# Two transformer blocks on one core: the adaptive modulation computed in three places, partly on VectorE

## Chip, core and metric

One core of a Trainium2 chip runs the whole kernel in a single launch. The metric is device time in microseconds, the median of several executions. TensorE multiplies matrices, VectorE and ScalarE do elementwise work and empty the accumulators, GpSimd does some elementwise work and issues some loads, SyncE issues the other loads. Matmul results go to eight accumulator banks.

## The reference

Two blocks run one after the other on 256 tokens of width 1024. The first block has a norm, a wide projection, a stick-breaking attention, an RWKV recurrence, gates over both, an output projection `w_o` and an FFN. The second block is modulated by a vector `c` that doesn't depend on the tokens:

```
def modulate(x, shift, scale):
    return rms_norm_2(x) * (1 + scale[:, None, :]) + shift[:, None, :]

# first block, cut
gates = sigmoid(proj[..., SB_COLS + RW_COLS:] + b_gate)
merged = gates[..., :D] * (o_sb @ w_sb_out) + gates[..., D:] * (o_rw @ w_rw_out)
x = x + rms_norm(merged @ w_o, norm_mix_post)
h = rms_norm(x, norm_ffn_pre)
x = x + rms_norm((silu(h @ w_ffn_gate) * (h @ w_ffn_up)) @ w_ffn_down, norm_ffn_post)
# second block, cut
mod = jax.nn.silu(c) @ w_ada + b_ada            # (1024) @ (1024 x 6144)
sh1, sc1, g1, sh2, sc2, g2 = jnp.split(mod, 6, axis=-1)
proj = modulate(x, sh1, sc1) @ w_in             # then pooling and a state space mixer
x = x + g1 * mix
x = x + g2 * hier_moe(modulate(x, sh2, sc2))    # 32 experts, two for each token
return rms_norm_2(x) * final_norm_w
```

## The kernel before

The code is written in the order of the computation, with tiles taken from pools. A scheduler that knows the dependences and the number of buffers then fixes an order of instructions for each engine before the launch; each engine works through its own list in that order and waits where an input or a buffer isn't ready. The stages are: first norm; projections of the RWKV part (`prw`); projections q, k and v of the attention (`pqk`, `pv`); attention, RWKV recurrence and gates (`pgate`, 16 column blocks) mixed with each other; output projections of both branches (`psb`, `prw`); `w_o` by rows with its norm (`fin_mix`); FFN in 22 groups (`pfg`, `pfu`); FFN down with its norm (`fin_ffn`); second block; router; 32 experts whose weights (192 MB) stream in.

Products in high precision are made from two rounded parts: `split_to` and `wsplit` have ScalarE cast a weight to `wh` and VectorE subtract to get `wl`, and `mm3` issues three matmuls.

`w_ada` is stored as 24 blocks of 256 columns, 1 MB each, with the 1024 rows as 8 groups of 128 in one tile. `mod_steps` handles a pair of blocks: GpSimd issues the two loads into the two buffers of the tag `wada`, TensorE makes 8 products for each block into a bank `pmod` (in four strips of 32 rows), ScalarE copies it to `modrow`, TensorE transposes the copy in four parts, and VectorE sums the four strips and adds `b_ada`. The result is four columns of `modT`, which holds the whole modulation as columns of 128. It is called twelve times: once after each of the four projections of q and k, and once after each of the eight gate weights `wg`.

Accumulator banks are split over three tags: m (`pm`), t (`pt_`) and s (`psm`). During the first block up to `w_o` m has two, t three and s three. Projections, `pmod` and half of the accumulators of `w_o` use m; attention scores `pz`, transposes `pwt`, attention outputs `po`, `prw` of the output projection and the other half of `w_o` use t; norms, RWKV and transposes use s. From the FFN on m and s have four each, and `pt_` takes m.

`dense_rows` runs a product over rows of the weight, keeps the last weights, finishes the first 128 tokens (`finish(0, ...)`), then multiplies the kept weights for the other 128, calls `fill` if there is one, and finishes them. For the FFN down product `fill` is `router_prep`, which prepares the router's bias and the rows `g2h` and `g1row`:

```
        finish(0, acc[0])
        for k, hi, lo in kept:
            go(1, k, hi, lo)
        if fill:
            fill()
        finish(1, acc[1])
```

Of the kernel before, what the change touches and what calls it, by code (L numbers as in the profile page):

```python
# [8 lines left out]
F32 = mybir.dt.float32  # L9
# [52 lines left out]
AFT = (9, 12)  # L62
SCW = 4
WARM = (16, 4, 5, 2, 9)
PN = "mttt"
XC, W1 = 512, 2
RWE = "pp" + "d" * 12
QE = "d" * 8
# [5 lines left out]
def two_blocks(ctx: ExitStack, tc: tile.TileContext, a: dict, out: bass.AP, dump=None, stop=""):  # L74
# [16 lines left out]
    def open_banks(*banks):  # L91
        if "pst" in ph:
            ph["pst"].close()
        ph["pst"] = ExitStack()
        ph["p"] = ph["pst"].enter_context(tc.tile_pool(name="psum%d" % banks[0], bufs=1, space=PSUM))
        ph["banks"] = banks
# [11 lines left out]
    def nm(s):  # L108
        uid[0] += 1
        return f"{s}{uid[0]}"  # L110
# [31 lines left out]
    def psm(s):  # L142
        return bank(s, 2)
# [7 lines left out]
    def pconst(s, shape, dt=F32):  # L151
        return ph["pool"].tile(shape, dt, tag=s, name=s, bufs=1)

    open_banks(2, 3, 3)
    open_phase("mixing")


# [9 lines left out]
    def row_bcast(s, src, q=sync):  # L167
        t = blk(s)
        q.dma_start(out=t, in_=src.to_broadcast([P, D]))
        return t  # L170
# [43 lines left out]
    def prm(name, i=0, n=1):  # L214
        o = sum(m for x, m in PARAMS[: [x for x, _ in PARAMS].index(name)])
        return par[:, o + i : o + i + n]
# [81 lines left out]
    def split_to(hi, lo, src, eng=dve):  # L298

        act.copy(hi, src)  # L300
        eng.tensor_tensor(lo, src, hi.bitcast(F32), ALU.subtract)  # L301
# [5 lines left out]
    def atv(t, k, c0=0, c1=256):  # L307
        return t[k // 4][:, (k % 4) * 256 + c0 : (k % 4) * 256 + c1]
# [68 lines left out]
    def mod_steps():  # L377


        i = mod_n[0]  # L380
        mod_n[0] += 2
        ps = pm("pmod")
        for b in range(2):
            t = ph["pool"].tile([P, 2048], F32, tag="wada", name=nm("wada"), bufs=2)
            pool.dma_start(out=t, in_=a["w_ada_2"][i + b])
            v = t.rearrange("p (k c) -> p k c", k=KC)
            for k in range(KC):
                g = k % 4
                pe.matmul(ps[32 * g : 32 * g + 32, b * 256 : b * 256 + 256], lhsT=csil[:, k : k + 1].to_broadcast([P, 32]), rhs=v[:, k], start=(k < 4), stop=(k >= 4))
        row = small("modrow", [P, 512], bufs=1)  # L390
        act.copy(row, ps)
        for q in range(4):
            pe.transpose(ps[:, q * P : (q + 1) * P], row[:, q * P : (q + 1) * P], ident)
        sm = small("mods", [P, 4])
        dve.tensor_reduce(sm, ps.rearrange("p (q g r) -> p q g r", q=4, g=4)[:, :, :, 0], axis=AX.X, op=ALU.add)
        dve.tensor_tensor(modT[:, 2 * i : 2 * i + 4], sm, prm("b_ada_2", 2 * i, 4), ALU.add)


    hT = act_T("hT")
# [414 lines left out]
    for g in range(8):  # L814
        v = load_cols(w_in, 13 + g, 256, KC, "wg")
        for j in range(2):
            ps = pm("pgate")
            dense_T(v, KC, hT, j, P, ps[:, :256], on(GTE, 2 * g + j))
            act.activation(hv(gt[g // 2], 2 * (g % 2) + j), ps[:, :256], AF.Sigmoid, bias=prm("b_gate", 2 * g + j))
        mod_steps()  # L820
    mT = act_T("mT", blk)
    for g in range(2):
        wsb = load_cols(a["w_sb_out"], g, 512, 4, "wsb")
# [97 lines left out]
        kept_o.append(0)  # L921
        return (gblk if len(kept_o) <= 8 else blk)(s_, F32R)

    dense_rows(a["w_o"], KC, mT, fin_mix, SO, keep_o, pos=PO)

    close_phase()

# [3 lines left out]
    NF = 22  # L931
    r2 = pconst("r2", [P, 256])
    fT = [[ph["pool"].tile([P, 1024], F32R, tag=f"f{i}{j}", name=f"f{i}{j}", bufs=1) for j in range(6)] for i in range(2)]
    for g in range(NF):
        t = raw("wff")
        sync.dma_start(out=t, in_=a["w_ffn"][g])
        vs = [t[:, j * 1024 : j * 1024 + 1024].rearrange("p (k c) -> p k c", k=KC) for j in range(2)]
        p1, p2 = pm("pfg"), pt_("pfu")
        dense_T(vs[0], KC, h2T, 0, P, p1[:, :256])
        dense_T(vs[1], KC, h2T, 0, P, p2[:, :256], alloc=lambda s_: blk(s_, F32R))  # L940
        while later:
            fin_mix2(*later.pop(0))
        sl = small("ffs", [P, 256], bufs=2)
        dve.tensor_tensor(sl, p1[:, :256], r2, ALU.mult)
        act.activation(sl, sl, AF.Silu)
        dve.tensor_tensor(sl, sl, p2[:, :256], ALU.mult)
        split_to(atv(fT[0], g), atv(fT[1], g), sl)
    gfp = row_bcast("gfp", a["norm_ffn_post"])


# [38 lines left out]
    def router_prep():  # L989
        ps = psm("prb")  # L990
        for k in range(KC):
            pe.matmul(ps[:, 0:40], lhsT=sh2(k).to_broadcast([P, P]), rhs=wrt[:, k], start=(k == 0), stop=(k == KC - 1))
        dve.tensor_tensor(rbias, rbias, ps[:, 0:40], ALU.add)
        pool.tensor_tensor(wrt, wrt, sc1p[:, 8:16].rearrange("p (k o) -> p k o", o=1).to_broadcast([P, KC, 40]), ALU.mult)

        ps = psm("prow")
        for j in range(4):
            for h in range(2):
                c = 40 + 4 * h + j
                pe.matmul(ps[64 * h : 64 * h + 64, j * P : (j + 1) * P], lhsT=modT[:, c : c + 1].to_broadcast([P, 64]), rhs=ident, start=True, stop=True)  # L1000
        act.copy(g2h, ps)
        g1.append(row_of("g1row", modT[:, 16:24]))
# [729 lines left out]
```

## Time and profile before

| | us |
|---|---|
| median of three runs (1136.47 to 1138.24) | 1136.75 |
| profiled execution | 1135.27 |
| its span | 1133.5 |
| TensorE busy | 1061.0 (94%) |
| VectorE busy | 569.6 (50%) |
| ScalarE busy | 406.5 (36%) |
| GpSimd busy | 80.2 (7%) |

Busy shares are averages over stages with different limits; what bounds a stage is read from the waits in that stage. TensorE has two lines, PE for matmuls and PEld for weight loads, and matmuls overlap each other, so the distance from one start to the next tells what one costs. A product of plain f32 data appears as two records.

### The profile page before, as it was taken

To read this page: it belongs to the slowest core of one execution; us is meant where nothing else is said; L and a number is where in the kernel's file an instruction comes from. 1 tells how busy PE (TensorE), PEld (TensorE's weight loads), DVE (VectorE), ACT (ScalarE), POOL (GpSimd) and SP (SyncE) were. 2 spreads that over 40 slices of the span, in tenths; PEclk is the share of its full clock that TensorE was granted. 3 is DMA by queue.
4 is the path that set the end of the run, shared out by engine and by line. 5 is a ranking of instruction groups with operands and counts; after the bars stand their busy time and mean duration, and the time that the engine had idled before them with its cause. 6 is when DMAs were issued, how large, how long until landed. Compare 5 with 4: busy or idle time off the path is not lost.

```text
span 1133.5 us, 17717 instructions
## 1 busy us (share of the span) xinstructions
PE 1061.0 (94%) x7134; PEld 736.8 (65%) x7134; DVE 569.6 (50%) x1164; ACT 406.5 (36%) x717; POOL 80.2 (7%) x155
## 2 busy tenths in 40 slices
PE   8999999889869999999999889999999999999995
PEld 7988777778769999887997653444444444433332
DVE  5576967527876664546795762322233322222213
ACT  5455343325354443443665541211112111111112
POOL 4001500000210000002400010000000000000000
PEclk9999999989889999999999999999999999999997
DMA  9654432583635555541854489999999999999993
GB/s 324 219 213 166 185 114 112 227 311 133 223 112 180 179 180 188 212 160 61 319 181 169 169 307 411 415 418 418 416 419 416 417 419 416 417 419 417 417 418 150
DMA packets 57718, 313.03 MB, mean 276 GB/s; under 512 B 8864, under 2 KB 11040, under 8 KB 28064
## 3 DMA queue, kind: packets, MB, share of 16 engines
q1 hardware_dynamic: 53712, 286.50, 64.9%
q0 software_dynamic: 3456, 25.17, 5.8%
q8 instruction: 58, 0.95, 0.3%
q10 hardware_dynamic: 464, 0.17, 0.1%
q14 instruction: 28, 0.23, 0.1%
HBM read 310.77 MB, written 1.05 MB: 275 GB/s over the span
## 4 chain that ended last, share of the span: by engine, by line
PE 66%; DMA 16%; DVE 8%; issue 7%; ACT 2%; POOL 1%; SPq 0%; DVEq 0%; POOLq 0%; ACTq 0%
PE ph L1479 14%; DMA wexp<-in_w_dram 11%; PE pyo L1542 7%; DMA wada<-in_w_ada_dram 4%; PE acc L331 3%; PE acc L332 3%; PE acc L330 3%; PE moe L1560 2%; DVE wl L301 2%; PE pga L1324 2%; PE pfg L330 2%; PE pfg L331 2%; PE pfg L332 2%; PE pfu L331 2%; PE pfu L330 2%
## 5 line engine op out<-in xcount | busy, mean ns | idle before, releaser
L1479 PE MATMUL ph<-wexp,xg 128*64 128x512 f32 x1024 | 229.2, 594 | 9.2 <-DMA wexp<-in_w_dram 8.7
L1479 PEld LDWEIGHTS ph<-wexp,xg 128*64 128x64 f32 x1024 | 71.9, 137 | 159.1 <-issue 129.8
L1542 PE MATMUL pyo<-wexp,gy 128*64 128x512 f32 x512 | 116.9, 598 | 2.6 <-DVE gy L1536 2.1
L1486 DVE TENSOR_TENSOR gy<-gy,ph 128x256 f32<-128x256 f32 x32 | 13.5, 421 | 151.6 <-ACT gy L1485 151.6
L1547 DVE SCALAR_TENSOR_TENSOR gy<-pyo,gs,g2h 128x512 f32<-128x512 f32 x32 | 24.0, 750 | 103.5 <-PE pyo L1542 103.5
L1542 PEld LDWEIGHTS pyo<-wexp,gy 128*64 128x64 f32 x512 | 34.1, 136 | 62.5 <-issue 54.2
L1485 ACT ACTIVATE gy<-ph 128x256 f32<-128x256 f32 x32 | 12.3, 385 | 164.3 <-PE ph L1479 164.3
L301 DVE TENSOR_TENSOR wl<-wff,wh 128x1024 fp32r<-128x1024 f32 x44 | 54.4, 1236 | 18.8 <-ACT wh L300 18.3
L301 DVE TENSOR_TENSOR wl<-wrows,wh 128x1024 fp32r<-128x1024 f32 (+1 forms) x42 | 49.5, 1197 | 24.6 <-ACT wh L300 24.4
L1551 ACT CAST yh<-gy 64x512 fp32r<-64x512 f32 x32 | 19.8, 618 | 115.6 <-DVE gy L1547 115.6
L300 ACT CAST wh<-wff 128x1024 fp32r<-128x1024 f32 x44 | 46.1, 1047 | 33.0 <-PE pfg L331 26.5
L300 ACT CAST wh<-wrows 128x1024 fp32r<-128x1024 f32 (+1 forms) x46 | 45.3, 1011 | 33.7 <-PE acc L331 21.6
L330 PE MATMUL pfg<-h2Th,wh 128*128 128x256 f32 x176 | 50.0, 284 | 0.1
L330 PE MATMUL pfu<-h2Th,wh 128*128 128x256 f32 x176 | 49.8, 283 | 0.0
L331 PE MATMUL pfu<-h2Tl,wh 128*128 128x256 f32 x176 | 49.8, 283 | 0.0
L332 PE MATMUL pfg<-h2Th,wl 128*128 128x256 f32 x176 | 49.8, 283 | 0.0
L331 PE MATMUL pfg<-h2Tl,wh 128*128 128x256 f32 x176 | 49.8, 283 | 0.0
L332 PE MATMUL pfu<-h2Th,wl 128*128 128x256 f32 x176 | 49.8, 283 | 0.0
L1324 PE MATMUL pga<-sel,hnh 128*128 128x256 f32 x128 | 33.1, 304 | 8.7 <-DVE sel L1318 7.0
L332 PE MATMUL pi<-h3Th,wl 128*128 128x256 f32 (+1 forms) x136 | 38.6, 284 | 1.8 <-DVE wl L301 1.8
L331 PE MATMUL pi<-h3Tl,wh 128*128 128x256 f32 (+1 forms) x136 | 38.5, 283 | 0.2 <-DVE h3Tl L326 0.2
L330 PE MATMUL pgate<-hTh,wh 128*128 128x256 f32 x128 | 38.7, 302 | 0.0
(549 smaller groups left out, 2574.5 us busy)
## 6 DMA issues: line engine op xcount, KB each, us to landing
wexp<-in_w_dram SPq DMA_DIRECT2D x134, 1024.0 KB, 15.0
wexp<-in_w_dram SPq DMA_DIRECT2D x116, 512.0 KB, 12.6
wada<-in_w_ada_dram POOLq DMA_DIRECT2D x24, 1024.0 KB, 6.8
wff<-in_w_ffn_dram SPq DMA_DIRECT2D x22, 1024.0 KB, 4.9
wrows<-in_w_ffn_down_dram SPq DMA_DIRECT2D x11, 1024.0 KB, 4.9
wg<-in_w_in_dram SPq DMA_DIRECT2D x8, 1024.0 KB, 4.9
wi<-in_w_in_dram SPq DMA_DIRECT2D x8, 1024.0 KB, 5.1
wrw<-in_w_in_dram SPq DMA_DIRECT2D x6, 1024.0 KB, 9.5
```

What stands on the lines that cost most here:

```text
L300: act.copy(hi, src)
L301: eng.tensor_tensor(lo, src, hi.bitcast(F32), ALU.subtract)
L330: pe.matmul(ps, lhsT=lh, rhs=rh, start=first, stop=False)
L331: pe.matmul(ps, lhsT=lh, rhs=rl, start=False, stop=False)
L332: pe.matmul(ps, lhsT=ll, rhs=rh, start=False, stop=last)
L1324: return pe.matmul(ps, lhsT=hn[tb][part][:, k * P : (k + 1) * P], rhs=sel[tb].rearrange("p (e j s) -> p e j s", e=GE, j=2)[:, :, 0, :], st ...
L1479: last = pe.matmul(ph_[64 * t_ : 64 * t_ + 64, :], lhsT=xg[k // 4][:, (k % 4) * 256 + el * CAP : (k % 4) * 256 + el * CAP + CAP], rhs=wa[k ...
L1486: dve.tensor_tensor(g, g, ph_[:, 256:512], ALU.mult)
L1542: last = pe.matmul(py_[64 * t_ : 64 * t_ + 64, :], lhsT=gT[:, (kc % 2) * P + (kc // 2) * 64 : (kc % 2) * P + (kc // 2) * 64 + 64], rhs=wb[ ...
L1547: dve.scalar_tensor_tensor(y32, py_, gs, g2h, op0=ALU.mult, op1=ALU.mult)
L1551: act.copy(y[hi], y32[hi])
L1560: last = pe.matmul(acc[tb][hf], lhsT=sT[:, tb * P : (tb + 1) * P], rhs=ys[hf], start=(e == 0), stop=(e == E - 1))
```

## The change

The twelve calls of `mod_steps` are split up. The four behind q and k stay. The eight in the gates stage go. Two stand in a `fill` of the `w_o` product, between the accumulation and the norm of the second 128 tokens. Two stand in `router_prep`, at the norm behind the FFN. The other eight blocks go through a new function `mod_late` in the FFN, one after every second group from group 4 to group 18: GpSimd issues the load, VectorE multiplies the eight row groups by their entries of `silu(c)` and adds them up in `msum`, and one group later TensorE sums `msum` over the partitions with a column of ones (`pmc`), two products with one column each; VectorE then adds `b_ada`. Banks up to `w_o` become three for m and two for t; a fourth bank of the first norm is taken from s in place of t.

```diff
-PN = "mttt"
+PN = "mttp"
...
-    open_banks(2, 3, 3)
+    open_banks(3, 2, 3)
...
+    def mod_late(i):
+
+
+        t = ph["pool"].tile([P, 2048], F32, tag="wada", name=nm("wada"), bufs=2)
+        pool.dma_start(out=t, in_=a["w_ada_2"][i])
+        v = t.rearrange("p (k c) -> p k c", k=KC)
+        s_ = ph["pool"].tile([P, 256], F32, tag="msum", name=nm("msum"), bufs=2)
+        dve.tensor_scalar(s_, v[:, 0], csil[:, 0:1], None, op0=ALU.mult)
+        for k in range(1, KC):
+            dve.scalar_tensor_tensor(s_, v[:, k], csil[:, k : k + 1], s_, op0=ALU.mult, op1=ALU.add)
+
+        def total():
+            ps = psm("pmc")
+            for q in range(2):
+                pe.matmul(ps[:, q : q + 1], lhsT=s_[:, q * P : (q + 1) * P], rhs=onec, start=True, stop=True)
+            dve.tensor_tensor(modT[:, 2 * i : 2 * i + 2], ps[:, 0:2], prm("b_ada_2", 2 * i, 2), ALU.add)
+
+        return total
...
             act.activation(hv(gt[g // 2], 2 * (g % 2) + j), ps[:, :256], AF.Sigmoid, bias=prm("b_gate", 2 * g + j))
-        mod_steps()
...
-    dense_rows(a["w_o"], KC, mT, fin_mix, SO, keep_o, pos=PO)
+    dense_rows(a["w_o"], KC, mT, fin_mix, SO, keep_o, pos=PO, fill=lambda: [mod_steps() for _ in range(2)])
...
+    total = None
     for g in range(NF):
...
         split_to(atv(fT[0], g), atv(fT[1], g), sl)
+        if total:
+            total()
+            total = None
+        if 4 <= g < 20 and g % 2 == 0:
+            total = mod_late(mod_n[0])
+            mod_n[0] += 1
+    if total:
+        total()
...
         pool.tensor_tensor(wrt, wrt, sc1p[:, 8:16].rearrange("p (k o) -> p k o", o=1).to_broadcast([P, KC, 40]), ALU.mult)
+        for _ in range(2):
+            mod_steps()
```

The scheduler's order shows where the moved work stands. First TensorE at the norm of `w_o`, before: the accumulation of the second 128 tokens ends, then come the transposes of the norm's result `xgf`, nine warming matmuls, and the first FFN group.

```order
L330 MATMUL acc_3305<-wh_3366,mTh_2952 128x512
L331 MATMUL acc_3305<-wl_3367,mTh_2952 128x512
L332 MATMUL acc_3305<-wh_3366,mTl_2954 128x512
L319 MATMUL ptr_3498<-ident,xgf_3295 128x128 x4
L319 MATMUL ptr_3505<-ident,xgf_3296 128x128 x4
L369 MATMUL warm_3512<-ident 128x128 x9
L330 MATMUL pfg_3545<-h2Th_3287,wh_3547 128x256
```

The same place on TensorE with the change:

```order
L332 MATMUL acc_3065<-wh_3126,mTl_2714 128x512
L389 MATMUL pmod_3237<-wada_3238,csil 32x256 x8
L389 MATMUL pmod_3237<-wada_3248,csil 32x256 x8
L393 MATMUL pmod_3237<-ident,modrow_3258 128x128 x4
L389 MATMUL pmod_3267<-wada_3268,csil 32x256 x8
L319 MATMUL ptr_3318<-ident,xgf_3055 128x128 x4
L389 MATMUL pmod_3267<-wada_3278,csil 32x256 x8
L319 MATMUL ptr_3325<-ident,xgf_3056 128x128 x4
L369 MATMUL warm_3332<-ident 128x128
L393 MATMUL pmod_3267<-ident,modrow_3288 128x128 x4
L369 MATMUL warm_3332<-ident 128x128 x8
L330 MATMUL pfg_3365<-h2Th_3047,wh_3367 128x256
```

One call stands ahead of the transposes, and the two blocks of the other stand one before each group of four.

Next VectorE in the FFN, with the change, from the first operation of the third summed block on (`wl` are subtractions for later weights, `ffs` and `f` the group's product and its split; before, the same rows stand there without those of `msum`):

```order
L405 TENSOR_SCALAR msum_4037<-wada_4035,csil 128x256
L407 SCALAR_TENSOR_TENSOR msum_4037<-wada_4035,csil,msum_4037 128x256
L301 TENSOR_TENSOR f_3358<-ffs_3812,f_3352 128x256
L407 SCALAR_TENSOR_TENSOR msum_4037<-wada_4035,csil,msum_4037 128x256 x2
L963 TENSOR_TENSOR ffs_3882<-pfg_3824,r_3350 128x256
L407 SCALAR_TENSOR_TENSOR msum_4037<-wada_4035,csil,msum_4037 128x256
L301 TENSOR_TENSOR wl_3974<-wff_3969,wh_3973 128x1024
L407 SCALAR_TENSOR_TENSOR msum_4037<-wada_4035,csil,msum_4037 128x256
L301 TENSOR_TENSOR wl_4226<-wff_4193,wh_4225 128x1024
L965 TENSOR_TENSOR ffs_3882<-ffs_3882,pfu_3825 128x256
L407 SCALAR_TENSOR_TENSOR msum_4037<-wada_4035,csil,msum_4037 128x256 x2
L301 TENSOR_TENSOR f_3358<-ffs_3882,f_3352 128x256
```

The eight operations of a block are spread over a group and a half. Those of the first two blocks stand earlier than in the code, among the first three groups.

Last TensorE at the norm behind the FFN, before (`prb` is the router's bias, `prow` the rows of `g2h` at L1000 and of `g1row` at L262, `ptr` the transposes with the shift at L315 and the norm's result at L321):

```order
L992 MATMUL prb_5509<-wrt,modT 128x40 x8
L1000 MATMUL prow_5520<-ident,modT 64x128 x8
L262 MATMUL prow_5531<-ident,modT 128x128
L321 MATMUL ptr_5469<-diag_5467,pn_5428 128x128 x4
L321 MATMUL ptr_5477<-diag_5467,pn_5428 128x128 x4
L262 MATMUL prow_5531<-ident,modT 128x128 x3
L262 MATMUL prow_5537<-ident,modT 128x128 x4
L315 MATMUL ptr_5584<-modT,ident 128x512
L315 MATMUL ptr_5592<-modT,ident 128x512
L321 MATMUL ptr_5584<-diag_5582,pn_5543 128x128 x4
L321 MATMUL ptr_5592<-diag_5582,pn_5543 128x128 x4
L330 MATMUL pi_5662<-h3Th_5056,wh_5663 128x256
```

With the change, on TensorE from the first transposes on (`prb`, the first block of the first call and one product of its second stand ahead of them):

```order
L321 MATMUL ptr_5417<-diag_5407,pn_5368 128x128 x4
L389 MATMUL pmod_5460<-wada_5471,csil 32x256 x7
L393 MATMUL pmod_5460<-ident,modrow_5481 128x128 x4
L389 MATMUL pmod_5490<-wada_5491,csil 32x256 x8
L1029 MATMUL prow_5520<-ident,modT 64x128
L262 MATMUL prow_5531<-ident,modT 128x128 x4
L262 MATMUL prow_5537<-ident,modT 128x128 x4
L315 MATMUL ptr_5584<-modT,ident 128x512
L389 MATMUL pmod_5490<-wada_5501,csil 32x256 x8
L321 MATMUL ptr_5584<-diag_5582,pn_5543 128x128 x4
L393 MATMUL pmod_5490<-ident,modrow_5511 128x128 x4
L315 MATMUL ptr_5592<-modT,ident 128x512
```

Behind these follow one transpose of `ptr_5592`, seven products of `prow_5520` that need the second call's result, three more transposes, and the first projection `pi`. From there on the lists of all engines agree with those of before, but for one matmul of `pi_5692` that no longer stands early.

## Rows read from the trace of the kernel before

**Rows 1.** Windows (us): length, busy PE, PEld, DVE, ACT, POOL, PEclk, DMA share, GB/s.

```profile
200.00:262.00 62.00, 55.69 (x522) 45.47 (x521) 22.41 (x46) 20.66 (x33) 5.30 (x10) 0.94 0.66 255
330.00:456.00 126.00, 125.97 (x1050) 125.97 (x1051) 74.03 (x112) 57.05 (x84) 0.00 (x0) 1.00 0.49 172
```

**Rows 2.** Waits of TensorE from 140 to 262 us: us in total, times, longest.

```profile
PE pmod L389 <- DMA wada<-in_w_ada_dram: 6.2, 3, 3.3
```

**Rows 3.** Timeline of TensorE, 236 to 241 us: start, length, instruction, idle before it.

```profile
236.57 1.93 PE L389 MATMUL pmod<-wada,csil 128*32 128x256 f32 x32
238.44 0.38 PE L330 MATMUL pgate<-hTh,wh 128*128 128x256 f32 x1
...
239.27 0.66 PE L393 MATMUL pmod<-ident,modrow 128*128 128x128 f32 x4
...
239.68 0.36 PE L330 MATMUL pgate<-hTh,wh 128*128 128x256 f32 x1
```

**Rows 4.** Timeline of TensorE in the v projection.

```profile
122.76 0.50 PE L330 MATMUL pv<-wh,hTh 128*128 128x512 f32 x1 [0.95 <-DVE mods L395]
```

**Rows 5.** Timeline of one attention head, 179 to 185 us.

```profile
179.28 0.48 PE L792 MATMUL pz<-kaT,qT 64*128 64x128 f32 x2
...
184.16 0.56 DVE L800 TENSOR_TENSOR sg<-sg,zm 128x385 f32<-128x385 f32 x1
```

**Rows 6.** Timeline of TensorE at the norm of w_o, and a window of it.

```profile
324.16 1.97 PE L319 MATMUL ptr<-ident,xgf 128*128 128x128 f32 x8 [8.70 <-DVE xgf L902]
325.92 4.05 PE L369 MATMUL warm<-ident 128*128 128x128 f32 x18
330.03 0.39 PE L330 MATMUL pfg<-h2Th,wh 128*128 128x256 f32 x1
...
330.37 0.28 PE L332 MATMUL pfg<-h2Th,wl 128*128 128x256 f32 x1
330.49 0.28 PE L330 MATMUL pfg<-h2Th,wh 128*128 128x256 f32 x1
...
324.00:330.00 6.00, 5.81 (x26) 5.51 (x26) 5.55 (x13) 3.55 (x7) 2.51 (x2) 0.51 0.15 64
```

**Rows 7.** Loads: chain pieces, a SyncE issue; by tile: landing, issue, ScalarE's copy.

```profile
145.33 5.11 DMA wada<-in_w_ada_dram
217.39 10.30 DMA wada<-in_w_ada_dram
317.85 0.33 SPq L936 DMA_DIRECT2D wff<-in_w_ffn_dram  x1
DMA to landing us min/median/max: 5.1/6.8/12.5
L385 POOL DMA_DIRECT2D wada<-in_w_ada_dram x14: 527/528/539, 145.3 to 250.7; - x14
L391 ACT COPY modrow<-pmod x12: 586/587/591, 67.3 to 259.7; 128x512 f32<-128x512 f32 x12
```

**Rows 8.** VectorE by form (busy us, mean ns, idle before); the last two in the FFN.

```profile
L517 DVE SCALAR_TENSOR_TENSOR kp<-rT,par,kp 128x256 f32<-128x256 f32 x4 | 1.9, 477 | 0.0
L499 DVE TENSOR_SCALAR ath<-ath,half_w 128x256 f32<-128x256 f32 x4 | 1.4, 345 | 0.4 <-ACT ath L473 0.4
...
L301 DVE TENSOR_TENSOR wl<-wff,wh 128x1024 fp32r<-128x1024 f32 x37 | 45.3, 1225 | 17.0 <-ACT wh L300 16.5
L944 DVE TENSOR_TENSOR ffs<-pfg,r 128x256 f32<-128x256 f32 x22 | 9.4, 425 | 20.5 <-PE pfg L332 19.0 <-ACT r L916 1.4
```

**Rows 9.** Timeline of TensorE: products with two columns, and what follows.

```profile
64.17 0.95 PE L243 MATMUL phs<-hind,kk 128*128 128x2 f32 x8
64.98 0.36 PE L332 MATMUL pqk<-hTh,wl 128*128 128x256 f32 x1
```

**Rows 10.** Timeline of TensorE at the norm behind the FFN.

```profile
521.55 1.87 PE L992 MATMUL prb<-wrt,modT 128*128 128x40 f32 x16
...
526.51 1.73 PE L262 MATMUL prow<-ident,modT 128*128 128x128 f32 x14
528.07 1.89 PE L315 MATMUL ptr<-modT,ident 128*128 128x512 f32 x4
532.24 2.05 PE L321 MATMUL ptr<-diag,pn 128*128 128x128 f32 x16 [2.29 <-DVE diag L295]
```

## The prediction, made before the result was known

> **What bounds the kernel now.** I read the busy times by stage first, then the chain that ended last, then the waits and the order in time of the stage that the change empties. The time before is a median of 1136.75 us; the profiled execution took 1135.27 us with a span of 1133.5 us, so 1.77 us lie around the span, and the median is 1.48 us above that execution. The sum below is made on the span, and both are added at the end.
>
> In the last part of the gates stage TensorE is busy for 55.7 of 62 us while VectorE is busy for 22.4 and ScalarE for 20.7; in the FFN TensorE has no idle time at all (125.97 of 126 us) and VectorE is busy for 74 us [rows 1]. So in both stages what TensorE does or waits for is the time. In the gates stage its only long waits are three for the blocks of `w_ada`, 6.2 us in all [rows 2]. From the second block's first projection on, the rows of all five engines stand in the same order as before, apart from one matmul of the first pair that moves by some rows; I therefore let everything behind that point shift as one piece. That holds for the expert stage too: its weights stream behind those same instructions, and nothing there starts by the clock.
>
> **What leaves the gates stage.** Eight of twelve calls of `mod_steps` leave it (sixteen blocks of 1 MB). Each call is 32 matmul records on TensorE, from 236.57 to the next gate matmul at 238.44, so 1.87 us, and later the transposes, from 239.27 to the next gate matmul at 239.68, 0.41 us [rows 3]. Eight calls give 8 x 2.28 = 18.2 us. The 6.2 us of waits for their blocks go with them [rows 2]: the eight gate weights that stay are 1 MB for some 6 us of matmuls (48 of them, 0.12 us each at the full clock [rows 6]), and VectorE and ScalarE have idle time there [rows 1], so I see nothing that takes the place of these waits. A third piece: at 122.76 the v projection waited 0.95 us for the sums of the fourth pair, which held one of two m banks [rows 4]; with three m banks the second v accumulator no longer needs that bank. Together 18.2 + 6.2 + 0.9 = 25.3 us less.
>
> **What the banks cost.** Three banks for m and two for t leave the attention one t bank for `po` and one through which scores and transposes of all heads pass in turn. A head takes from its scores at 179.28 to the product at 184.16 + 0.56, so 5.4 us [rows 5], and in the new order some 28 to 39 gate matmuls (3.4 to 4.7 us) or work of the RWKV states stand between them on TensorE. So the cover mostly suffices, and one head lies open by up to 2 us. I take 1.5 us for the eight heads; the bounds are 0 (all covered) and 5 (two more heads open by 1.7 us).
>
> **The norm behind w_o.** Two calls now stand in TensorE's wait of 8.70 us before the transposes at 324.16 [rows 6]. The accumulation ends at 324.16 - 8.70 = 315.46. The first call's blocks were loaded long before; its matmuls end at 317.3. The second call's blocks go into the same two buffers, so they can only be issued when the first call has read each: about 316.5 and 317.4. A load alone landed in 5.11 us, one among three in 10.30, and a load of `wff` goes out at 317.85 [rows 7]. I take 7 us for the first (323.5) and 9 for the second (326.4). The first half then fits ahead of the transposes, which also come some 0.6 us later because ScalarE copies the first call's row (0.59 us) [rows 7] in between; the second half ends at 327.3, the second transposes at 328, the second call's own transposes at 328.7 behind another copy. [...]
>
> **The FFN.** Eight blocks are weighted and summed on VectorE: one multiplication by a column and seven multiply-adds, the nearest rows being 345 ns and 477 ns for 128x256 [rows 8]. That is 0.345 + 7 x 0.477 = 3.7 us a block and 29.5 us in all. VectorE had 74 of 126 us busy [rows 1], so it ends at some 104: hidden, as long as the sums fill its waits. The rows of the new order say that they can: the multiply-adds stand between ScalarE's casts and the subtractions that wait for them. Four banks let `ffs` lag by more than a group of 5.8 us. On TensorE each block adds two products with a single column. Four products of the nearest kind (128x2) took from 64.17 to 64.98 [rows 9], so two take 0.41 us and eight pairs 3.2 us; nothing covers them, since TensorE never idles there. One place is tight: the sums of the first block stand ahead of the first group's product on VectorE, while their load is issued only at about 327.5, behind an addition on GpSimd that ends the norm. It lands at 333 to 338, and VectorE is there at about 332.5. I take 0.5 us for TensorE, bounds 0 and 6.
>
> **The norm behind the FFN.** Here TensorE goes from the router's bias at 521.55 through the rows of `g2h` and `g1row` to the last transposes at 532.24, after a wait of only 2.29 us [rows 10]. Two calls come in between, again through two buffers. By the new order: bias until 523.4, first block's eight products until 524.5, first transposes until 526.7, the rest of the first call until 527.2, its own transposes at 528.2 to 528.7 behind ScalarE's copy. The third block is issued at 524.5 and lands alone after 5.11 us at 529.6, its products end at 530.6; one row product and the rows of `g1row` (1.73 us) until 532.5, the shift (half of 1.89) until 533.4, the last block's products until 534.4, four transposes until 535.4, the second call's transposes until 535.8, the next shift and a transpose until 536.9. Then seven row products wait for VectorE's sum of the second call until about 537.2, and the last three transposes end near 538.6, where they ended at 534.3 (532.24 + 2.05). That is 4.3 us; I take 4.5. Lower bound 2 (two calls of 2.28 less some 2.3 of idle time), upper bound 10 (both loads at 10.30 us).
>
> **The sum.** -25.3 + 1.5 + 1.5 + 3.2 + 0.5 + 4.5 = -14.1 us: a span of 1119.4, with 1.77 an execution of 1121.2, with 1.48 a median of **1122.7 us**. The two ends that can meet most easily, attention and both norms at their low ends, give 1117; a few terms near their high ends give 1129.
>
> **The rivals.** *The transfers show at both norms.* The loads there are issued late by construction. For it speaks the 10.30 us row [rows 7]; against it, that nothing else is loading at the second norm, where it needs more than twice the lone load. Price: +3 more at the first, +5.2 more at the second, some 1 at the first sums: 1132.
>
> *VectorE becomes the bound of the FFN.* This one ends on the other side. VectorE works in order, and its waits in the FFN are short (ScalarE's casts, 16.5 us; TensorE, 19.0 us [rows 8]). If the sums lie beside these waits instead of in them, all 29.5 us show on TensorE: -14.1 - 0.5 + 29.5 = +14.9, so 1151.7. The kernel is slower once more than (14.6 + 2.3) / 8 = 2.1 us of a block's 3.7 show. Against it: the order puts them into the waits, and the banks allow a lag.
>
> *Attention lies open.* If each of the eight heads shows the 2 us by which 3.4 us of cover miss 5.4 us, that is 16 us instead of 1.5: 1137.2, no change. Against it: five heads have 4.3 us or more of other work in the order.
>
> *Loads starved by VectorE.* GpSimd issues all these loads, now in the stage where VectorE works most. The slowest of the 24 landings took 12.5 us, the median 6.8 [rows 7]. If the first two FFN loads land so late, VectorE holds up some 4 us more of the FFN's start, and each norm gains 1: about 1128. [...]
>
> **How the numbers follow.** A measurement of this kernel tells about 0.2% (2.3 us) from no change. Forecast, 1117 to 1129: 0.75. Transfers, 1132: 0.11. Starved loads, 1128: 0.05. Attention open, 1137: 0.05. VectorE bound, 1152: 0.04. The range 1117 to 1132 takes in the first three. Faster 0.91, same 0.05, slower 0.04.
>
> **What would show it.** Right: no wait for `wada` between 140 and 240 us; `psb` starts some 24 us earlier; the FFN takes 3 to 4 us more from its first to its last matmul, with no TensorE idle time; the stretch between accumulation and first projection of the second block grows by 4 to 5 us; everything later shifts. Wrong: `pgate` waits for `wg` or for `pwt`; `pfg` or `pfu` waits for VectorE's `wl` or `ffs`; a wait for `wada` at a norm of more than 5 us; or the expert stage ends at another distance from the second block's first projection.

## The result, and the profile after

The changed kernel takes 1121.11 us (median of 4 runs, 1118.02 to 1123.37) against 1137.49 for the kernel before beside it (4 runs): a ratio of 0.985, 95% interval 0.983 to 0.987. The forecast was 1122.7 us. Its profiled execution took 1120.24 us, 1118.5 of them span. VectorE is busy for 592.2 us of it (569.6 before), TensorE for 1053.5 (1061.0).

The windows that answer to [rows 1], in the same columns, one in the last gates and one in the FFN:

```profile
200.00:232.00 32.00, 31.41 (x249) 29.18 (x248) 21.52 (x41) 14.14 (x23) 0.00 (x0) 1.00 0.35 112
330.00:430.00 100.00, 100.00 (x839) 100.00 (x838) 75.69 (x139) 43.99 (x65) 3.18 (x6) 1.00 0.67 246
```

TensorE now has almost no idle time in the last gates, and its granted clock is 1.00 there where it was 0.94. Over the whole stage, from the first gate matmul to the first `psb`, the clock is 0.97 in both kernels: the changed one has a stretch at the lower clock in the attention instead (0.50 from 150 to 154 us), behind a wait of 1.1 us. In the window of the FFN TensorE still never idles, and VectorE is busy for 76% instead of 59%.

The waits of TensorE from 118 to 290 us (total, times, longest):

```profile
PE prw L332 <- DVE wl L301: 3.3, 1, 3.3
PE pv L331 <- DVE wl L301: 2.2, 1, 2.2
```

No wait for `wada` is left [rows 2]. New is 2.2 us in the v projection for a subtraction on VectorE, where a wait of 0.95 us for a bank stood [rows 4].

The norm of w_o on TensorE, to be read beside [rows 6]:

```profile
287.45 1.93 PE L389 MATMUL pmod<-wada,csil 128*32 128x256 f32 x32
290.63 0.66 PE L393 MATMUL pmod<-ident,modrow 128*128 128x128 f32 x4 [1.24 <-ACT modrow L391]
294.38 1.88 PE L389 MATMUL pmod<-wada,csil 128*32 128x256 f32 x16 [3.10 <-DMA wada<-in_w_ada_dram]
296.44 1.12 PE L319 MATMUL ptr<-ident,xgf 128*128 128x128 f32 x4 [0.17 <-DVE xgf L920]
299.46 1.07 PE L389 MATMUL pmod<-wada,csil 128*32 128x256 f32 x16 [1.91 <-DMA wada<-in_w_ada_dram]
...
301.80 1.95 PE L369 MATMUL warm<-ident 128*128 128x128 f32 x16
303.81 0.39 PE L330 MATMUL pfg<-h2Th,wh 128*128 128x256 f32 x1
```

The first transposes wait for almost nothing of their own; the second call waits for its two loads, 3.10 and 1.91 us. The warming matmuls run at 0.12 us a record (1.95 us for 16), where before they took 0.23 (4.05 us for 18), at a granted clock of 0.51 [rows 6].

One summed block in the FFN on TensorE, and the row behind it:

```profile
340.07 0.50 PE L412 MATMUL pmc<-onec,msum 128*128 128x1 f32 x4
340.44 0.36 PE L330 MATMUL pfg<-h2Th,wh 128*128 128x256 f32 x1
```

The sums on VectorE, by form, from 300 to 436 us (busy, mean ns, idle before):

```profile
L407 DVE SCALAR_TENSOR_TENSOR msum<-wada,csil,msum 128x256 f32<-128x256 f32 x56 | 26.7, 481 | 0.7
L405 DVE TENSOR_SCALAR msum<-wada,csil 128x256 f32<-128x256 f32 x8 | 2.8, 347 | 0.6 <-DMA wada<-in_w_ada_dram 0.6
```

They take 29.5 us, just the sum that was made from rows of other operations [rows 8], and wait only 0.6 us for loads.

The norm behind the FFN, beside [rows 10]:

```profile
499.90 1.87 PE L1019 MATMUL prb<-wrt,modT 128*128 128x40 f32 x16
...
506.86 0.66 PE L393 MATMUL pmod<-ident,modrow 128*128 128x128 f32 x4 [0.70 <-ACT modrow L391]
508.58 1.07 PE L389 MATMUL pmod<-wada,csil 128*32 128x256 f32 x16 [1.07 <-DMA wada<-in_w_ada_dram]
...
518.13 0.37 PE L330 MATMUL pi<-h3Th,wh 128*128 128x256 f32 x1
```

The third block comes 1.07 us late, about as large a wait as the forecast had it (0.9); most of the rest of the added time is work of the calls.

**Stages.** The table gives times between seven marks on TensorE, read from each kernel's timeline: first gate matmul, end of the w_o accumulation, first and last matmul of the FFN's groups, router's bias, first `pyt` in the second block, first `ph` of the experts. The rows from e1 on are the experiments below; e11 is the changed kernel again. Each row is one execution, and e1 to e4, e5 to e8 and e9 to e12 ran on three different chips, so a difference of 1 to 2 us between two rows can come from the execution.

| us | start of gates at | gates to w_o | norm of w_o | FFN | down product | norm, second block to pyt | pyt to ph |
|---|---|---|---|---|---|---|---|
| before | 132.85 | 182.62 | 14.56 | 127.40 | 64.12 | 111.19 | 39.46 |
| changed | 133.76 | 153.77 | 16.28 | 132.10 | 63.99 | 116.47 | 41.02 |
| e1 none | 133.23 | 154.85 | 13.49 | 127.40 | 64.16 | 112.19 | 41.01 |
| e2 FFN | 132.38 | 153.13 | 13.83 | 131.56 | 64.26 | 112.24 | 39.49 |
| e3 w_o | 133.84 | 152.47 | 18.88 | 127.41 | 63.61 | 111.20 | 39.46 |
| e4 router | 134.62 | 152.93 | 13.93 | 127.42 | 63.97 | 117.65 | 39.46 |
| e5 banks | 133.91 | 183.47 | 13.14 | 127.41 | 63.61 | 112.18 | 41.05 |
| e6 old banks | 132.62 | 152.53 | 16.32 | 132.23 | 63.94 | 118.06 | 39.51 |
| e7 FFN 12 | 132.79 | 153.51 | 18.07 | 137.80 | 63.67 | 112.21 | 40.89 |
| e8 FFN 16 | 134.05 | 154.04 | 14.16 | 144.52 | 63.47 | 111.18 | 39.47 |
| e9 no load | 131.52 | 172.10 | 14.44 | 127.41 | 63.78 | 111.19 | 39.46 |
| e10 mix | 135.43 | 157.61 | 14.58 | 133.28 | 64.17 | 111.18 | 39.46 |
| e11 changed again | 133.98 | 153.51 | 18.39 | 132.05 | 63.99 | 116.48 | 39.51 |
| e12 mix, old banks | 144.34 | 160.42 | 14.54 | 132.20 | 64.03 | 112.22 | 39.48 |

Up to the end of the w_o accumulation the change wins 27.9 us (0.9 lost ahead of the gates, 28.8 won behind); the norm of w_o gives back 1.7, the FFN 4.7, the norm behind it 5.3, and the second block 1.6.

### The profile page after: what moved, and what is told of

Its sections match the earlier page's. It is cut to its first block, busy times and chain, and to the rows that moved or that the text cites. A ratio compares the mean times of both kernels' runs of the same rounds, so it can differ in the third digit from the quotient of the medians.

```text
span 1118.5 us, 17553 instructions
## 1 busy us (share of the span) xinstructions
PE 1053.5 (94%) x7022; PEld 732.2 (65%) x7022; DVE 592.2 (53%) x1228; ACT 403.6 (36%) x713; POOL 82.0 (7%) x155
## 4 chain that ended last, share of the span: by engine, by line
PE 73%; DMA 15%; DVE 7%; ACT 2%; issue 2%; POOL 1%; SPq 0%; DVEq 0%; POOLq 0%; ACTq 0%
PE ph L1508 15%; DMA wexp<-in_w_dram 11%; PE pyo L1571 7%; PE acc L331 3%; PE acc L332 3%; PE acc L330 3%; PE moe L1589 2%; PE pga L1353 2%; DVE wl L301 2%; PE pfg L330 2%; PE pfg L331 2%; PE pfg L332 2%; PE pfu L331 2%; PE pfu L330 2%; PE pfu L332 2%
## 5 line engine op out<-in xcount | busy, mean ns | idle before, releaser
L301 DVE TENSOR_TENSOR wl<-wff,wh 128x1024 fp32r<-128x1024 f32 x44 | 55.1, 1253 | 17.2 <-ACT wh L300 17.1
L1353 PE MATMUL pga<-sel,hnh 128*128 128x256 f32 x128 | 33.1, 305 | 8.7 <-DVE sel L1347 7.0
L330 PE MATMUL pi<-h3Th,wh 128*128 128x256 f32 (+1 forms) x136 | 38.6, 284 | 0.0
```

Of the source, the lines that this page charges most:

```text
L330: pe.matmul(ps, lhsT=lh, rhs=rh, start=first, stop=False)
L1353: return pe.matmul(ps, lhsT=hn[tb][part][:, k * P : (k + 1) * P], rhs=sel[tb].rearrange("p (e j s) -> p e j s", e=GE, j=2)[:, :, 0, :], st ...
```

## The experiments

**The parts one by one.** All four start from the changed kernel, clear `modT` at the start, and keep only some of its new places:

```diff
+    dve.memset(modT, 0.0)                # all four
-    dense_rows(..., fill=lambda: [mod_steps() for _ in range(2)])
+    dense_rows(...)                      # e1, e2, e4
-        if 4 <= g < 20 and g % 2 == 0:
+        if False:                        # e1, e3, e4
-        for _ in range(2):
-            mod_steps()                  # e1, e2, e3
```

> The change with its twelve other blocks and calls left out: the eight calls are gone from the gates, the banks are changed, and nothing stands in their place at the norm of w_o, in the FFN or in the router's preparation. Left out of the computation: 16 of the 24 blocks of the modulation, whose columns stay zero. Theory (the terms add up): everything up to the end of the w_o accumulation comes 27 to 28 us earlier than before, as in the changed kernel, the norm of w_o, the FFN and the norm behind it last as before to within 0.5 us, and the span is 1105 to 1107 us, or 1104 to 1109 with the step in the second block. Rival (the moved work interacts with the gates, by its loads or buffers): the gates give only the 23.8 us of the prediction, span 1109 to 1110, or a stage behind them differs from before by over 1 us.

Measured: ratio 0.9741 (0.970 to 0.978), span 1107.0. Up to the end of the w_o accumulation 27.4 us earlier; the FFN is unchanged to 0.01 us. The norm of w_o is 1.1 us shorter and the stretch behind the FFN 1.0 longer than before, so the theory holds for the gates and the sum, and its bound of 0.5 us was too tight for the two stages with a long wait in them. By its letter the rival's second condition, a stage that differs by over 1 us, is met too (the norm of w_o, and the second block by 1.5). But the same stage differs as much without any moved work: the norm of w_o takes 14.56 us before and 13.14 in e5.

> The same with the eight summed blocks in the FFN alone; left out: eight blocks of the modulation. Theory: the FFN lasts 4.0 us longer than before (eight pairs of single-column products at 0.50 us), and 0.2 less than in the changed kernel or more, since no call at the norm of w_o delays the first block's load; the other stages as in the kernel with nothing moved; span 4 us above that one. Rival (the multiply-adds on VectorE show, beyond their 0.9 us wait): the FFN lasts 4.7 us longer or more even without the calls at the norm.

Measured: the FFN 4.16 us longer, 0.54 less than in the changed kernel; the wait at its start is 0.37 us here and 0.92 there, so the calls at the norm of w_o do delay the first block. Less that wait, either kernel gives 3.8 us for eight pairs, 0.47 each. The total of 2751.93 us says nothing of the change: with this modulation more tokens go to one expert than its place holds, and a second path behind the experts (its first matmul at 1102.7 us) takes the rest.

> The same with the two calls behind the w_o accumulation alone; left out: twelve blocks of the modulation. Theory: from the end of that accumulation to the first FFN matmul 1.7 us more than before (16.3 instead of 14.6 us), with waits for the second call's blocks of about 3 and 2 us and the warming matmuls at the full clock; FFN as before. Rival (the warming matmuls' clock is not due to the calls): they take 4 us again, and the norm 2.5 us more.

Measured: 1110.22 us, ratio 0.9765 (0.974 to 0.979). The norm takes 18.88 us, 4.3 more than before. The waits are as expected (2.94 and 1.84 us), but the sixteen warming records take 2.90 us, between the 1.95 of the changed kernel and 4 us. Windows from the last block of the calls to the first FFN matmul, of the changed kernel and of e3:

```profile
299.00:304.00 5.00, 4.48 (x43) 3.56 (x44) 3.19 (x8) 4.06 (x7) 1.56 (x3) 1.00 0.38 154
298.00:305.00 7.00, 6.83 (x42) 5.49 (x42) 3.88 (x11) 4.88 (x9) 1.34 (x2) 0.56 0.23 96
```

So neither theory holds: the same work is found at a granted clock of 1.00 and of 0.56.

> The same with the two calls in the router's preparation alone; left out: twelve blocks of the modulation. Theory: from the router's bias to the second block's first projection some 5.3 us more than before, the calls' own TensorE time of 4.6 us and about 1 us of wait for the third block, all else as before. Rival (the FFN's loads on the same queue and in the same buffers delayed the calls): 4 us or less here, since the buffers are free from the start.

Measured: 1113.02 us, ratio 0.979 (0.977 to 0.981). The stretch from the router's bias is 6.5 us longer than before (6.9 up to the second block's first projection), with waits for the loads of 0.45 and 1.10 us. So the rival falls: the price belongs to the calls, and no load of the FFN delayed them. The 5.3 us of the theory are missed, in an order that is not that of the changed kernel: here row products stand before the last block, and TensorE also waits 0.62 us for VectorE's sum.

**The banks.** e5 puts the new banks into the kernel before, e6 the old ones into the changed kernel:

```diff
-PN = "mttt"
+PN = "mttp"
-    open_banks(2, 3, 3)
+    open_banks(3, 2, 3)
```

> The kernel before with the banks alone changed: three for m, two for t, and the fourth bank of the first norm from s. All twelve calls stay in their places. Theory of the prediction: attention lies open by about 1.5 us, the v projection's wait of 0.95 us goes: within 1 us of before. Rival 1 (the banks are what gave the 2 to 4 us that the gates stage won beyond the prediction): 2 to 4 us faster. Rival 2 (attention open): up to 16 us slower.

> The change with the banks of before (two for m, three for t). Theory: 0 to 1 us slower than the changed kernel, the 0.95 us wait of the v projection back and little else. Rival 1 (the banks gave the surplus in the gates): the stage up to the end of the w_o accumulation 2 to 4 us longer. Rival 2 (two t banks cost as predicted): about 1 us faster than the changed kernel, since attention has three banks again.

Measured: e5 1.0007 of before (0.9992 to 1.0023), its w_o accumulation ending 1.9 us later. e6 0.985 of before (0.982 to 0.987), the accumulation 30.3 us earlier than before, where eight executions of the new banks (changed, e1 to e4, e7, e8, e11) have 27.4 to 30.0, 28.4 in the mean. Both point to a cost of some 2 us for the new banks up to there, by one execution each and against a spread of 2.6 us among the eight; it is little enough to vanish in the total. Rival 1 of both falls, and of the expectations for e6 rival 2 is nearest. Little of it lies in the attention: from the first gate matmul to the first `psb` e5 takes 0.6 us longer than before, and e6 takes 98.1 us where the eight have 97.7 to 99.2. More lies ahead of the gates, which start 1.1 us later in e5. The v projection shows why its 0.95 us were not won: e5 also waits there for VectorE, 2.1 us. VectorE was busy for 15.29 of the 16 us from 118 to 134 in the kernel before, so a freed bank only moves TensorE's wait to the next subtraction. Windows of before, of e5, and of e2, which waits 2.4 us there:

```profile
118.00:134.00 16.00, 14.99 (x96) 11.28 (x85) 15.29 (x35) 6.60 (x9) 13.02 (x26) 1.00 0.38 131
118.00:134.00 16.00, 13.91 (x56) 10.54 (x54) 14.68 (x32) 4.92 (x7) 13.02 (x23) 0.89 0.72 262
118.00:134.00 16.00, 13.65 (x67) 10.63 (x66) 15.42 (x37) 6.18 (x7) 10.80 (x21) 1.00 0.39 131
```

All nine of these executions with the new banks (the eight and e5) wait 2.1 to 2.4 us for this subtraction. Six of them (changed, e3, e4, e5, e8, e11) then show 0.89 and start the gates at 133.8 to 134.6; e1, e2 and e7 show 1.00 and start them at 132.4 to 133.2, about as the kernel before. So the larger wait costs time ahead of the gates mainly where the lower clock follows it.

**More blocks on VectorE.** e7 sums twelve blocks in the FFN and drops the calls in the router's preparation; e8 sums all sixteen and drops those at the norm of w_o too:

```diff
-        if 4 <= g < 20 and g % 2 == 0:
+        if 2 <= g < 20 and g % 3:        # e7
+        if 3 <= g < 19:                  # e8
```

> The change with twelve blocks summed on VectorE in the FFN and no call in the router's preparation; the two calls at the norm of w_o stay. Theory (the sums are hidden, only the products on TensorE and the calls count): the FFN 2 us longer than in the changed kernel (four more pairs at 0.50 us), the norm behind it 5.3 us shorter: 3.3 us faster, about 1118 us. Rival (VectorE shows, busy for 115 of 133 us): TensorE waits in the FFN for subtractions or products on VectorE, 3 us or more in all, and nothing is won.

> The change with all sixteen blocks summed on VectorE in the FFN, one behind each of sixteen groups, and no call at either norm. Theory (hidden sums): the FFN 4 us longer than in the changed kernel, the two norms 1.7 and 5.3 us shorter: 3 us faster. Rival (VectorE bound, 130 of 134 us busy): the FFN lasts 138 us or more, with waits of TensorE for VectorE, and the kernel is no faster than the changed one, or slower.

Measured: e7 1118.99 us, 0.985 of before (0.982 to 0.988); e8 1121.73, 0.987 (0.984 to 0.989). Neither differs measurably from the changed kernel. e7's FFN is 10.4 us longer than before, of which twelve pairs are 5.6. Of the other 4.8 us, 3.5 are these waits of TensorE, listed from 302 to 450 us:

```profile
PE pfu L330 <- DVE ffs L965: 1.3, 2, 0.8
PE pr L933 <- DVE rsy L288: 1.1, 1, 1.1
PE pfg L332 <- DVE wl L301: 1.1, 2, 0.6
```

In e8 it is 17.1 us longer, sixteen pairs being 7.5. The waits there, and the clock around the two longest:

```profile
PE pmc L412 <- DVE msum L407: 4.6, 3, 2.3
```

```profile
370.00:390.00 20.00, 17.70 (x125) 17.53 (x124) 14.11 (x31) 6.15 (x9) 1.36 (x3) 0.83 0.71 264
390.00:410.00 20.00, 18.24 (x141) 18.07 (x141) 15.68 (x34) 6.90 (x10) 1.23 (x3) 0.91 0.74 265
```

The wait of 2.3 us is followed by a granted clock of 0.83, one of 1.8 us by 0.91; that is 0.17 x 20 + 0.09 x 20 = 5.2 us of clock, and with 7.5 for the pairs and 4.6 for the waits it makes 17.3. VectorE's busy time of some 130 us, as reckoned, would fit in beside 134 us of TensorE as a sum; as an order it doesn't. So the rival in which VectorE becomes the bound exists. In these orders it begins between ten and twelve blocks: the ten of e10, below, make the FFN 5.9 us longer, 4.7 for their pairs and 1.2 besides, hardly more than eight do.

**The calls without their waits.** e9 is the kernel before, with the eight calls in the gates on the two blocks that are there:

```diff
-    def mod_steps():
+    def mod_steps(load=True):
...
+            if load:
+                t = ph["pool"].tile([P, 2048], F32, tag="wada", name=nm("wada"), bufs=2)
+                pool.dma_start(out=t, in_=a["w_ada_2"][i + b])
+                kept_w.append(t)
+            t = kept_w[-2 + b] if not load else t
...
-        mod_steps()                      # in the gates
+        mod_steps(False)
```

> The kernel before with all its twelve calls in their places, but the eight calls in the gates load nothing: they multiply the two blocks that the fourth call loaded. Left out: the loads of sixteen blocks, whose columns of the modulation are those of other blocks. Theory (a wait costs twice): the three waits for the blocks, 6.2 us, go, and with them the two stretches at half the clock behind them, in which the trace of before shows a granted clock of 0.91 from 220 to 240 us and 0.92 from 240 to 262 us, 0.09 x 20 + 0.08 x 22 = 3.6 us; so the stage up to the end of the w_o accumulation is 8.5 to 11 us shorter, with the clock at 1.00 in the last gates. Rival (the clock there follows the calls themselves, their f32 products): 5 to 7 us shorter and the clock at 0.95 or below.

Measured: the accumulation ends 11.9 us earlier (10.5 of it from the gates' start on), and the clock is 1.00 from 118 to 262 us. (Its total of 2767.71 us holds the second path of e2 again.) Windows of the kernel before around its longest wait:

```profile
224.00:228.00 4.00, 0.67 (x12) 0.20 (x8) 1.22 (x1) 0.74 (x2) 0.53 (x1) 0.94 0.73 266
228.00:232.00 4.00, 4.00 (x31) 2.78 (x24) 0.25 (x2) 0.59 (x1) 0.53 (x1) 0.63 1.03 414
```

The same windows of e9:

```profile
224.00:228.00 4.00, 4.00 (x36) 4.00 (x35) 0.99 (x3) 1.42 (x2) 0.00 (x0) 1.00 0.75 262
228.00:232.00 4.00, 4.00 (x50) 2.88 (x49) 1.80 (x2) 2.01 (x3) 0.00 (x0) 1.00 0.02 4
```

In 224 to 228 TensorE waits; in 228 to 232 it is busy throughout, at 0.63, where e9 has 1.00. The calls are the same in both kernels, so here the lower clock goes with the wait and not with their f32 products: the theory holds, the rival falls. (e9 takes away the loads together with the waits; what the loads do besides isn't separated.) The 11.9 us are more than the 9.8 worked out, and outside the 8.5 to 11 expected. By parts, the gates start 1.3 us earlier, from there to the first `psb` it is 9.2 us less, in the output projections 1.8 less, and in the w_o product 0.5 more. So in the stage for which the 9.8 were reckoned the sum is nearly right. Windows of the output projections, before and in e9:

```profile
258.17:291.30 33.13, 28.29 (x217) 26.14 (x214) 28.38 (x48) 14.87 (x25) 9.37 (x5) 0.91 0.42 149
247.65:278.96 31.31, 26.73 (x201) 25.06 (x197) 27.09 (x46) 14.46 (x24) 9.51 (x5) 0.95 0.42 146
```

Of their 1.8 us the clock makes up 0.09 x 33.1 - 0.05 x 31.3 = 1.4. Why the gates start earlier stays open.

**Another split.** e10 sums four blocks in the gates and ten in the FFN, with one call at the norm of w_o; e12 sums six and eight, with the old banks (the second argument of `mod_late`, new here, gives the sums in the gates one buffer):

```diff
-        if 4 <= g < 20 and g % 2 == 0:
+        if 2 <= g < 22 and g % 2 == 0:   # e10
-    dense_rows(..., fill=lambda: [mod_steps() for _ in range(2)])
+    dense_rows(..., fill=lambda: mod_steps())
-        for _ in range(2):
-            mod_steps()
+        if total:                        # in the gates
+            total()
+            total = None
+        if g % 2:                        # e10; e12: g < 6
+            total = mod_late(mod_n[0], 1)
+            mod_n[0] += 1
```

> The change with other places for the sixteen blocks: four summed on VectorE in the gates (one buffer for the sums there), one call at the norm of w_o, ten blocks summed in the FFN, none in the router's preparation. Theory (each summed block costs its two products, 0.50 us, and the rest hides): the gates 2 us longer than in the changed kernel, the norm of w_o 1 to 2 us shorter, the FFN 1 us longer, the norm behind it 5 to 6 us shorter: 3 to 5 us faster than the changed kernel. Rival (VectorE in the gates or in the FFN is late): waits of TensorE for weights split on VectorE in either stage, 3 us or more, and nothing won.

> The changed kernel itself, beside the others of this group, as their measure. Theory (single executions differ by where stretches at half the clock fall): total again 0.983 to 0.988 of before, but the stages differ from the first trace by 1 to 2 us at one or two places where TensorE waited just before. Rival (the stages' times belong to the kernel): the same stage times to within 0.3 us.

> As the mix above, but with the banks of before (two for m, three for t), six blocks summed in the gates and eight in the FFN. Theory: the same price for each block wherever its sums hide, so the same time as the mix above to within 1 us, and 3 to 5 us faster than the changed kernel. Rival (VectorE is the limit in the gates and output projections): 2 us or more slower than the mix above, with waits for weights split on VectorE.

Measured, side by side: e10 1117.62 us, 0.984 of before (0.982 to 0.986); e11 1120.27, 0.986 (0.984 to 0.988); e12 1128.93, 0.995 (0.993 to 0.997). e10 has the lowest median, 2.7 us below the changed kernel's, but the intervals overlap. Of its theory the norms hold: one call at the norm of w_o is nearly free (14.58 us against 14.56), and the norm behind the FFN is as before. The gates do not: with four blocks the w_o accumulation ends some 6 us later than without, instead of 2. The waits for VectorE there are 2.9 us in the v projection and 3.4 in the output projections, hardly more than the 2.2 and 3.3 of the changed kernel, so they explain less than 1 us of it; where the rest is from stays open.

e11's median is within a microsecond of the changed kernel's 1121.11 us, but its norm of w_o is 2.1 us longer than in the first profiled execution and its second block 1.5 us shorter: the stages of one execution are good to 1 or 2 us, as that theory has it.

e12 shows what a misplaced sum does. Timelines of GpSimd and VectorE:

```profile
129.54 1.15 POOL L402 DMA_DIRECT2D wada<-in_w_ada_dram  x2 [0.36 <-issue]
...
134.77 0.35 DVE L405 TENSOR_SCALAR msum<-wada,csil 128x256 f32<-128x256 f32 x1 [9.00 <-DMA wada<-in_w_ada_dram]
...
135.29 1.21 DVE L301 TENSOR_TENSOR wl<-wv,wh 128x1024 fp32r<-128x1024 f32 x1
```

Waits of TensorE in the same stretch:

```profile
PE pv L331 <- DVE wl L301: 9.7, 1, 9.7
```

GpSimd issues the first load only after its part of the RWKV inverse, at 129.54; VectorE has reached the first sum at 125.8 and stands before it for 9 us, with the next subtraction of the v projection queued behind; TensorE waits for that subtraction for 9.7 us.

## Why the prediction was right, and where it was off

The total was forecast as -14.1 us on the span; it was -15.0 in the changed kernel's first profiled execution and -14.3 in the second (e11). By its steps:

- **Gates.** Forecast -25.3 + 1.5 = -23.8, measured -27.9 up to the end of the w_o accumulation. The first `psb`, which the prediction took as its sign ("some 24 us earlier"), starts 25.3 us earlier. The calls were sized well: e6 less e9, both with the old banks, gives 30.3 - 11.9 = 18.4 us for eight, against 18.2. What was mis-sized is the term "-6.2" for the waits: without them e9 needs 9.2 us less between the first gate and `psb`, since each of the two longer waits was followed by a stretch at half the clock (0.50 from 228 to 230 us and from 248 to 250; 0.91 from 220 to 240 us, 0.92 from 240 to 262, 3.6 us lost in all), and the window of [rows 1] already had 0.94 in its clock column. A stage that the forecast had no term for adds to it: the output projections take 29.4 us at a granted clock of 0.97 instead of 33.1 at 0.91, while the w_o product takes 1.0 us more.
- **The bank in the v projection.** The term "-0.9" was wrong: VectorE was the limit there. With the new banks TensorE waits 2.1 to 2.4 us instead of 0.95, and the gates start 0.5 us earlier to 1.8 later than before, 0.7 later in the mean of eight executions.
- **Attention.** The term "+1.5" was too large: from the first gate to `psb` the old and the new banks differ by 0.6 us in e5 and by 0.1 between e6 and the mean of the eight, so its lower bound, all covered, was nearest. Together with the v projection it gave +0.6, against some 2 us measured: the one term was too large, the other had the wrong sign. Attention doesn't lie open, so that rival (1137) falls; no wait of it for `pwt` or `po` is longer than 1.1 us.
- **Norm of w_o.** +1.5 forecast, +1.7 measured, but +3.8 and +4.3 in e11 and e3. Five executions with two calls there have 16.3 to 18.9 us, 17.6 in the mean; seven without calls have 13.1 to 14.6, 13.9 in the mean. So no run shows the term +1.5 as a price of its own: the executions showed some 3.6 us in its place, and the near hit of the first one is luck. The loads came about as late as reckoned; the price went with the granted clock there: the sixteen warming records took 1.95 us in the changed kernel, at 1.00 from 299 to 304 us, and 2.90 us in e3, at 0.56 from 298 to 305.
- **FFN.** +3.7 forecast, +4.7 measured: 0.47 us a pair instead of 0.41, and 0.9 instead of 0.5 us for the late first sums. VectorE's 29.5 us were hidden as read from the order.
- **Norm behind the FFN.** +4.5 forecast, +5.3 measured (also in e11), 6.5 in e4, with another order, and 6.9 in e6, with a granted clock of 0.89 from 500 to 516 us (sixteen records of `prow` take 3.18 us there, 2.05 in the changed kernel). The rival in which the transfers show at both norms stays away: the third block's wait was 1.07 us.
- **The rest.** Forecast as a rigid shift. It was one in e11; in the first execution 1.6 us came up in the second block, which the last section takes up.
- **Starved loads.** With VectorE at 76%, GpSimd's part of a load in the FFN took 527 to 567 ns (527 to 539 in the gates before [rows 7]); the eight loads there landed after 5.1 to 6.9 us, and the landings of all 24 loads had a median of 5.3 us (6.8 before [rows 7]). Nothing in these rows is held up, so this rival falls.

That the terms' errors were of both signs (-4.1 in the gates, +0.2, +1.0, +0.8 and +1.6 behind) made the total better than its parts; that the median came within 2 us of the forecast is luck to that extent. What holds without luck is the mechanism: the work of the calls leaves a stage that TensorE bounds, and the sums are hidden in the FFN.

## What to carry to other kernels

Price a wait of TensorE with the clock that follows it: read the granted clock in the windows behind the wait, and add what it loses there (0.63 in the four microseconds behind the longest wait of the kernel before, 3.3 us). Not every wait was followed by the lower clock: behind that of 2.1 to 2.4 us in the v projection it came in six executions of nine (0.89 from 118 to 134 us). Work moved to an engine that is busy for 59% of a stage is free only as long as it fits between the waits in that engine's order; here ten sums of 3.7 us did, but for a wait of some 1 us at the start, and twelve no longer did. A gap holds as much foreign work as its loads can be ready for: one call at the norm of w_o cost some 0.6 us (14.6 us, against 13.1 to 14.6 without, 13.9 in the mean), a second that had to load through the same two buffers cost 2 to 4 us.

## What was not expected of the hardware

The same code shows stretches at the lower clock in different places from one execution to the next. In the second block the orders of before and after are equal. Windows of the kernel before (PEclk is the third figure from the end):

```profile
632.00:635.00 3.00, 1.94 (x9) 1.54 (x10) 3.00 (x7) 3.00 (x5) 0.00 (x0) 0.79 0.20 30
635.00:638.00 3.00, 2.49 (x7) 1.53 (x5) 3.00 (x8) 0.78 (x3) 0.00 (x0) 0.64 0.89 336
```

Of the changed kernel, some 5 us later in the program (the first `pyt` starts at 632.74 before and at 616.37 in the changed kernel):

```profile
621.00:624.00 3.00, 2.31 (x6) 1.81 (x7) 2.72 (x13) 0.62 (x2) 0.00 (x0) 0.70 0.99 366
624.00:627.00 3.00, 3.00 (x12) 2.36 (x11) 0.86 (x1) 0.00 (x0) 0.00 (x0) 0.73 0.81 309
```

The clock lost is the same, (0.21 + 0.36) x 3 = 1.7 us and (0.30 + 0.27) x 3 = 1.7 us. Before, it fell where TensorE waited for VectorE now and then (busy for 4.43 of the 6 us), and cost little; in the changed kernel it fell later, mostly on dense matmuls (5.31 of 6 us), and the stage was 1.6 us longer. In e2, e3, e4 and e11 the stage has its old length; of the fourteen executions ten have 39.5 us and four 40.9 to 41.1. Of a change of a few microseconds, one profiled execution can therefore misplace 1 to 2 us.
